# Attention: where the probabilities are divided by their sum

## The chip, the cores and the metric

The kernel runs on one core of one Trainium2 chip. Its time is the device time of one execution in microseconds (us). Beside the times stands one profiled execution, taken by the hardware profiler; its rows are used below. The engines are named as the profile names them: PE (TensorE matmul; PEld is its weight load), DVE (VectorE), ACT (ScalarE), POOL (GpSimd) and SP, which issues the weight transfers. Each engine works through its own instructions in the order in which the program holds them, and an instruction that waits holds back everything behind it on that engine.

## What is computed

Two blocks are chained over one sequence of 256 tokens with 1024 features. The first has convolutions and a mixture of experts; the change doesn't touch it. The second has two layers, each a feed-forward part, a mixer with three attentions of eight heads ("a" dilated, "b" banded with a sink, "c" over selected keys), and another feed-forward part. The step that the change touches is the same in all three attentions:

```python
p = jnp.exp(s - m[..., None])
den = p.sum(-1)
if sink is not None:
    den = den + jnp.exp(sk - m)
o = jnp.einsum('nbgrqk,nbkgd->nbqgrd', p.astype(v.dtype), vb, ...)
o = o / den.transpose(0, 1, 4, 2, 3)[..., None]
```

## The kernel before

The weights come from memory in 1 MB units through a helper that splits each into a high and a low half of 16 bits: ACT writes the high half (L120, 128x2048), DVE the low half (L107). The large projections run on PE with those halves (L1592, three terms).

In a mixer the projections of one layer come one after the other in a fixed list, and after the matmuls of each projection one **turn** of attention work is issued. The order in a turn is written out by hand: the projection's matmuls (L1592), the ACT half of the next weight unit (L120), work left over from an earlier turn (`flush`, L1768 and L1770), what the projection's result needs (`take`: the rotation on DVE, L1740 to L1743, and a copy to 16 bits on ACT, L1751), then `tick`, then the DVE half of the weight unit (L107), then `settle`. For the narrow projections `kc` and `kb` the ACT half comes after `take` and not before it.

An **item** is one attention, one block of 128 queries (c = 0 or 1) and four heads. There are 12 items in a layer, 24 in all; an item of the second query block (c = 1) has 256 keys in place of 128, so twice the probabilities. An item goes through four steps, spread over three turns:

- `soft`: scores on PE (L1840), addition of the mask on DVE into `pq` (L1893), row maximum (L1895), its negative `nm` (L1900), the exponentials on ACT in place, with their sums into `den` (L1902). `pq` lies with the queries on the partitions.
- `settle`, at the end of the same turn: the reciprocal of `den` on DVE (L1919).
- `flip`, in the next turn: transposes of `pq` on PE (L1930), their copy to `pT` on ACT (L1931), and four matmuls that spread the reciprocals over the rows of the values (L1937), copied to `div` on ACT (L1940).
- `values`, in the turn after: the matmuls with the values (L1954), the product with `div` on DVE into `o` (L1960), its high half `oh` on ACT (L1962), its low half `ol` on POOL (L1963).

`tick` issues `values` of the oldest item, `flip` of the middle one and `soft` of a new one, in this order. So on PE a flip's transposes stand after the values' matmuls and before the scores of the next item.

Of the kernel before, what the change touches and what calls it, by code (L numbers as in the profile page):

```python
# [10 lines left out]
F32 = mybir.dt.float32  # L11
# [3 lines left out]
AF = mybir.ActivationFunctionType  # L15
OP = mybir.AluOpType
# [3 lines left out]
P = 128  # L20
# [5 lines left out]
XS = 4.0  # L26
# [141 lines left out]
class Kernel:  # L168
# [958 lines left out]
    def experts(self, l, rank, w2, lp, later):  # L1127
# [111 lines left out]
        for j in range(17):  # L1239
            if j < 16:  # L1240
                pg = first("g", j)
                if j > 1:
                    scatter(j - 2)
                if j:
                    flip(j - 1)
                else:
                    back(0)
                pu = first("u", j)
                s = mp.tile([P, 512], F32, name="sil")
                nc.scalar.activation(s, pg, AF.Silu)  # L1250
                hid[j] = mp.tile([P, 512], F32, name="hid")
                nc.vector.scalar_tensor_tensor(hid[j], pu, WS[j // 2][:, j % 2 : j % 2 + 1], s, op0=OP.mult, op1=OP.mult)  # L1252
            else:
                scatter(j - 2)
                flip(j - 1)
# [448 lines left out]
class Attention:  # L1704
# [179 lines left out]
    def soft(self, x, c, hs):  # L1884
        nc, pool, kn = self.nc, self.pool, self.kn
        den = pool.tile([P, 4], F32, name="den", bufs=4)
        nm = pool.tile([P, 4], F32, name="nm", bufs=4)
        bias = self.sel[c] if x == "c" else kn.bias[x, c]
        kof = {"a": lambda h: h, "b": lambda h: h // 4, "c": lambda h: 0}[x]
        banks, nk, per = self.scores("q" + x, "k" + x, c, hs, kof)  # L1890
        pq = pool.tile([P, 4, S], F32, name="pq", bufs=3)[:, :, :nk]
        for n, bank in enumerate(banks):
            nc.vector.tensor_tensor(pq[:, n * per : n * per + per], bank.rearrange("p (j s) -> p j s", j=per),  # L1893
                                    bias[:, None].to_broadcast([P, per, nk]), op=OP.add)
        nc.vector.tensor_reduce(nm, pq, axis=AX.X, op=OP.max)  # L1895
        if x == "b":
            nc.vector.scalar_tensor_tensor(nm, nm, SOFT, self.sink[:, hs : hs + 4], op0=OP.mult, op1=OP.max)
            nc.vector.tensor_scalar(nm, nm, -1.0, None, op0=OP.mult)
        else:
            nc.vector.tensor_scalar(nm, nm, -SOFT, None, op0=OP.mult)  # L1900
        for j in range(4):
            nc.scalar.activation(pq[:, j], pq[:, j], AF.Exp, scale=SOFT, bias=nm[:, j : j + 1],  # L1902
                                 accum_out=den[:, j : j + 1])
        sk = None
        if x == "b":
            sk = pool.tile([P, 4], F32, name="sk", bufs=4)
            nc.vector.tensor_add(sk, self.sink[:, hs : hs + 4], nm)
            nc.scalar.activation(sk, sk, AF.Exp)
        self.state[x, c, hs] = (pq, den, sk)
        self.open = (den, sk)  # L1910

    def settle(self):

        if self.open:
            den, sk = self.open
            self.open = None
            if sk is not None:
                self.nc.vector.tensor_add(den, den, sk)
            self.nc.vector.reciprocal(den, den)  # L1919

    def flip(self, x, c, hs):

        nc, pool, kn = self.nc, self.pool, self.kn
        pq, den, sk = self.state[x, c, hs]
        out = []
        for s in range(c + 1):
            pt = kn.acc()
            pT = pool.tile([P, 512], F32, name="pT", bufs=4)
            for j in range(4):
                nc.tensor.transpose(pt[:, j * P : j * P + P], pq[:, j, s * P : s * P + P], kn.ident)  # L1930
            nc.scalar.activation(pT, pt, AF.Copy)  # L1931
            out.append(pT.rearrange("p (i e q) -> p i e q", e=2, q=P))

        pt = kn.ps()
        for j in range(4):
            i, e = divmod(j, 2)
            nc.tensor.matmul(pt[64 * e : 64 * e + 64, i * P : i * P + P], den[:, j : j + 1].to_broadcast([P, 64]), kn.ident,  # L1937
                             start=True, stop=True)
        div = pool.tile([P, 2 * P], F32, name="div", bufs=2)
        nc.scalar.activation(div, pt[:, : 2 * P], AF.Copy, scale=XS)  # L1940
        self.state[x, c, hs] = (out, div)

    def values(self, x, c, hs):

        nc, pool, kn = self.nc, self.pool, self.kn
        pT, div = self.state.pop((x, c, hs))
        v = self.v[x]
        pt = kn.ps()
        n = 1 if x == "a" else 2
        for i in range(0, 2, n):  # L1950
            for s in range(c + 1):
                for e in range(2):
                    v0 = {"a": (hs + 2 * i + e) * 64, "b": hs // 4 * 64, "c": 0}[x]
                    nc.tensor.matmul(pt[64 * e : 64 * e + 64, i * P : (i + n) * P].rearrange("p (i q) -> p i q", i=n),  # L1954
                                     v[:, s, v0 : v0 + 64], pT[s][:, i : i + n, e], start=(s == 0), stop=(s == c))
        if (c, hs) == (0, 0):
            self.oT[x] = tuple(pool.tile([P, 4, S], F16, name=n, bufs=2) for n in ("oh", "ol"))
        h, lo = (t[:, hs // 2 : hs // 2 + 2, c * P : c * P + P] for t in self.oT[x])
        o = pool.tile([P, 2 * P], F32, name="o", bufs=2)
        nc.vector.tensor_tensor(o, pt[:, : 2 * P], div, op=OP.mult)  # L1960
        o = o.rearrange("p (i q) -> p i q", i=2)
        nc.scalar.activation(h, o, AF.Copy)  # L1962
        nc.gpsimd.tensor_tensor(lo, o, h, op=OP.subtract)  # L1963


@with_exitstack
# [48 lines left out]
```

## Time and profile before

| | us |
|---|---|
| median of 3 runs | 2457.27 (2452.61 to 2458.95) |
| the profiled execution, its own time | 2455.99 |
| span of its trace, first to last instruction | 2454.3 |
| PE busy, of the span | 2345.2 (96%) |
| DVE busy | 1227.5 (50%) |
| ACT busy | 897.1 (37%) |
| POOL busy | 107.4 (4%) |

The two mixers lie at about 1440 to 1680 us and 2030 to 2270 us of the span. The busy shares are means over stages with different limits: what a change in the mixers is worth is read from the mixers alone, and there from which wait ends last. All times in rows are from the start of the span. A timeline row gives the start, the length, the engine, the line, the operation with what it writes and reads, and, where the engine sat idle before it, for how long and what ended that.

### The profile page before, as it was taken

What the parts mean: (1) busy time and instruction counts of PE and PEld (TensorE: products, weight loads), DVE (VectorE), ACT (ScalarE), POOL (GpSimd) and SP (SyncE); (2) the same over time, 40 slices, a digit from 0 to 9 for tenths busy, and PEclk for the clock granted to TensorE, in tenths of its full rate; (3) what the DMA queues carried; (4) which work ended last, traced back from release to release, by engine and by line L of the source; (5) the groups of instructions that cost most, each with busy time, mean ns of one, the idle gap of its engine ahead of it and who ended that gap; (6) DMA issues with size and microseconds to landing.
All of it is one profiled execution on the core that took longest, in us unless ns stands there. A gap on an engine that the chain in (4) does not pass through costs nothing.

```text
span 2454.3 us, 38061 instructions
## 1 busy us (share of the span) xinstructions
PE 2345.2 (96%) x16219; PEld 1383.2 (56%) x16219; DVE 1227.5 (50%) x1910; ACT 897.1 (37%) x1222; POOL 107.4 (4%) x169
## 2 busy tenths in 40 slices
PE   7989999999999999999979999999999999999998
PEld 5534343443386443334448855547888875554985
DVE  2775122111277222111157486968557567877654
ACT  2342111111143211111134447675444445676442
POOL 0100000000000000000020011110000002110000
PEclk8999999999999999999999999999999999999999
DMA  8977999999998999999976544536656555445651
GB/s 273 405 317 318 421 421 421 421 421 421 414 362 322 377 420 421 421 421 421 420 296 228 173 168 172 189 138 231 216 172 241 197 173 176 139 160 183 246 167 67
DMA packets 191033, 709.91 MB, mean 289 GB/s; under 512 B 15054, under 2 KB 50382, under 8 KB 134026
## 3 DMA queue, kind: packets, MB, share of 16 engines
q1 hardware_dynamic: 187850, 698.50, 73.7%
q10 hardware_dynamic: 3008, 8.92, 1.1%
q8 instruction: 129, 2.11, 0.3%
q14 instruction: 46, 0.38, 0.0%
HBM read 706.33 MB, written 1.05 MB: 288 GB/s over the span
## 4 chain that ended last, share of the span: by engine, by line
PE 50%; DMA 8%; issue 4%; DVE 4%; ACT 1%; POOL 0%; ACTq 0%; DVEq 0%; SPq 0%; POOLq 0%
PE ps L1470 18%; PE ps L1592 9%; PE ps L1198 6%; PE acc L1450 5%; DMA w<-in_e_w_up 3%; DMA w<-in_e_w_gate 3%; PE acc L1431 3%; PE ps L1220 2%; DVE w L107 1%; DMA w<-in_e_w_down 1%; PE acc L1692 1%; PE ps L1152 1%; PE ps L1954 1%; PE acc L1840 1%; PE acc L1236 1%
## 5 line engine op out<-in xcount | busy, mean ns | idle before, releaser
L107 DVE SCALAR_TENSOR_TENSOR w<-w,w 128x2048 f16<-128x2048 f32 (+3 forms) x239 | 525.6, 2213 | 234.8 <-ACT w L120 234.4
L120 ACT ACTIVATE w<-w 128x2048 f16<-128x2048 f32 (+3 forms) x239 | 434.6, 1832 | 251.5 <-PE ps L1470 140.0
L1470 PEld LDWEIGHTS <-w 128*128 128x128 f16 x4992 | 461.2, 112 | 11.4 <-issue 2.0
L1470 PE MATMUL ps<-xh,w 128*128 128x256 f16 (+1 forms) x3328 | 378.5, 257 | 1.1 <-DVE w L107 1.0
L1252 DVE SCALAR_TENSOR_TENSOR hid<-ps,ws,sil 128x512 f32<-128x512 f32 x32 | 24.0, 751 | 476.1 <-PE ps L1198 476.1
L1198 PE MATMUL ps<-w,xl 128*64 128x512 f32 x1024 | 240.4, 599 | 15.7 <-DMA w<-in_e_w_gate 15.6
L1198 PE MATMUL ps<-w,xh 128*64 128x512 f32 x1024 | 238.9, 595 | 14.8 <-DMA w<-in_e_w_gate 12.1
L1220 PE MATMUL ps<-w,hT 128*64 128x512 f32 x1024 | 237.0, 596 | 7.1 <-DMA w<-in_e_w_down 4.0
L1470 PE MATMUL ps<-xl,w 128*128 128x256 f16 (+1 forms) x1664 | 222.9, 257 | 1.9 <-DVE xl L333 1.9
L1592 PE MATMUL ps<-w,xh 128*128 128x512 f16 (+2 forms) x896 | 195.3, 362 | 0.5 <-ACT xh L332 0.5
L1198 PEld LDWEIGHTS ps<-w,xh 128*64 128x64 f32 x1024 | 80.0, 137 | 156.8 <-issue 121.2
L1198 PEld LDWEIGHTS ps<-w,xl 128*64 128x64 f32 x1024 | 78.4, 137 | 158.8 <-issue 120.1
L1220 PEld LDWEIGHTS ps<-w,hT 128*64 128x64 f32 x1024 | 80.3, 137 | 139.1 <-issue 111.0
L1227 ACT ACTIVATE yh<-y 128x512 f16<-128x512 f32 x64 | 40.3, 630 | 259.7 <-DVE y L1226 259.7
L1592 PEld LDWEIGHTS <-xh 128*128 128x128 f16 x896 | 85.4, 98 | 85.6 <-issue 2.4
L1226 DVE TENSOR_TENSOR y<-ps,g 128x512 f32<-128x512 f32 x64 | 44.0, 688 | 169.7 <-PE ps L1220 169.7
L1208 ACT ACTIVATE hT<-ps 128x512 f32<-128x512 f32 x32 | 19.1, 597 | 272.2 <-PE ps L1206 272.2
L1450 PE MATMUL acc<-w,hh 128*128 128x512 f16 x384 | 114.2, 379 | 0.0
L1592 PE MATMUL ps<-w,xl 128*128 128x512 f16 (+2 forms) x448 | 106.1, 362 | 0.0
L1431 PE MATMUL acc<-w,hh 128*128 128x512 f16 x320 | 95.2, 379 | 0.0
L1450 PE MATMUL acc<-w,hl 128*128 128x512 f16 x192 | 72.8, 379 | 0.0
L1592 PEld LDWEIGHTS <-xl 128*128 128x128 f16 x448 | 43.5, 98 | 45.7
(392 smaller groups left out, 2853.5 us busy)
## 6 DMA issues: line engine op xcount, KB each, us to landing
w<-in_e_w_gate SPq DMA_DIRECT2D x128, 1024.0 KB
w<-in_e_w_up SPq DMA_DIRECT2D x128, 1024.0 KB
w<-in_e_w_down SPq DMA_DIRECT2D x128, 1024.0 KB
w<-in_ffn_in SPq DMA_DIRECT2D x80, 1024.0 KB
w<-in_w_in SPq DMA_DIRECT2D x50, 1024.0 KB
w<-in_ffn_out SPq DMA_DIRECT2D x44, 1024.0 KB
w<-in_ada_w SPq DMA_DIRECT2D x40, 1024.0 KB
w<-in_b_w_in SPq DMA_DIRECT2D x12, 1024.0 KB
```

Of the source, the lines that this page charges most:

```text
L107: self.nc.vector.scalar_tensor_tensor(h[:, 1, :n], t[:, :n], WS, h[:, 0, :n], op0=OP.mult, op1=OP.subtract)
L120: self.nc.scalar.activation(h[:, 0, :n], t[:, :n], AF.Copy, scale=WS)
L1152: nc.tensor.matmul(pt[:, e * P : e * P + P], t[:, c, k + e :: 8], o[:, c], start=(i == c == 0), stop=(i == c == 1))
L1198: nc.tensor.matmul(pt[64 * e : 64 * e + 64], XT[j][:, 4 * h + k, 64 * e : 64 * e + 64], W[e][:, k * 512 : k * 512 + 512], start=(h == 0 an ...
L1220: nc.tensor.matmul(banks[n][64 * e : 64 * e + 64], hT[j][:, 2 * h + i, 64 * e : 64 * e + 64], W[e][:, i * D + n * 512 : i * D + n * 512 + ...
L1226: nc.vector.tensor_mul(y[:, sl], banks[n], G[:, sl])
L1227: nc.scalar.activation(yh[:, sl], y[:, sl], AF.Copy, scale=XS)
L1236: nc.tensor.matmul(accs[c][n], t, y[:, n * 512 : n * 512 + 512], start=False, stop=(j == 15 and i == 1), skip_group_check=True)
L1431: nc.tensor.matmul(accs[c][n], H[tx][:, 2 * h + f, c * P : c * P + P], ho[:, tw, f * D + n * 512 : f * D + n * 512 + 512], start=(j == 0 a ...
L1450: nc.tensor.matmul(accs[c][n], H[tx][:, 2 * h + f, c * P : c * P + P], ho[:, tw, f * D + n * 512 : f * D + n * 512 + 512], start=(j == 0 a ...
L1470: nc.tensor.matmul(pt[:, f % 2 * S + t0 : f % 2 * S + t1], h[:, tw, k * n + f : (k + 1) * n : nf], X[tx][:, 4 * (q % 2) + k, t0:t1], start ...
L1592: nc.tensor.matmul(pt[:, :n], X[tx][:, nk * q + k, c * P : c * P + P], h[:, tw, k * n : k * n + n], start=(q == 0 and k == 0 and tx == tw ...
```

## The change

The probabilities are multiplied by the reciprocals of their sums on DVE while they still lie by query, in `settle`. The four matmuls that spread the reciprocals and the copy `div` go. `oh` is then made by ACT straight from the matmuls' result, and `ol` by DVE from the same result and `oh`; the product with `div` and the subtraction on POOL go.

```diff
@@ soft
-        self.state[x, c, hs] = (pq, den, sk)
-        self.open = (den, sk)
+        self.state[x, c, hs] = pq
+        self.open = (pq, den, sk)
@@ settle
             self.nc.vector.reciprocal(den, den)
+            self.nc.vector.tensor_tensor(pq, pq, den[:, :, None].to_broadcast([P, 4, pq.shape[2]]), op=OP.mult)
@@ flip
-        pt = kn.ps()
-        for j in range(4):
-            i, e = divmod(j, 2)
-            nc.tensor.matmul(pt[64 * e : 64 * e + 64, i * P : i * P + P], den[:, j : j + 1].to_broadcast([P, 64]), kn.ident,
-                             start=True, stop=True)
-        div = pool.tile([P, 2 * P], F32, name="div", bufs=2)
-        nc.scalar.activation(div, pt[:, : 2 * P], AF.Copy, scale=XS)
-        self.state[x, c, hs] = (out, div)
+        self.state[x, c, hs] = out
@@ values
-        o = pool.tile([P, 2 * P], F32, name="o", bufs=2)
-        nc.vector.tensor_tensor(o, pt[:, : 2 * P], div, op=OP.mult)
-        o = o.rearrange("p (i q) -> p i q", i=2)
-        nc.scalar.activation(h, o, AF.Copy)
-        nc.gpsimd.tensor_tensor(lo, o, h, op=OP.subtract)
+        o = pt[:, : 2 * P].rearrange("p (i q) -> p i q", i=2)
+        nc.scalar.activation(h, o, AF.Copy, scale=XS)
+        nc.vector.scalar_tensor_tensor(lo, o, XS, h, op0=OP.mult, op1=OP.subtract)
```

On DVE, from the end of the turn that makes the second item to the mask of the third, these rows stood before (`rr`, `rq`: the rotation of the next projection; `acc`: the scores' result):

```order
L1919 RECIPROCAL den<-den 128x4
L1740 TENSOR_TENSOR rr<-ps,sind 128x8x32 x2
L1742 TENSOR_TENSOR rq<-ps,cosd 128x512
L1743 TENSOR_TENSOR rq<-rq,rr 128x512
L1960 TENSOR_TENSOR o<-ps,div 128x256
L1893 TENSOR_TENSOR pq<-acc,bias_a_9758 128x512 x2
```

The same place on DVE now:

```order
L1919 RECIPROCAL den<-den 128x4
L1920 TENSOR_TENSOR pq<-pq,den 128x4x128
L1740 TENSOR_TENSOR rr<-ps,sind 128x8x32 x2
L1742 TENSOR_TENSOR rq<-ps,cosd 128x512
L1743 TENSOR_TENSOR rq<-rq,rr 128x512
L1954 SCALAR_TENSOR_TENSOR ol<-ps,oh 128x2x128
L1893 TENSOR_TENSOR pq<-acc,bias_a_9758 128x512 x2
```

The multiplication L1920 has come in ahead of the rotation, and in the place of L1960, which read results of PE and `div`, stands L1954, which reads `oh` of ACT, ahead of the mask L1893.

On ACT, in the turn of the projection `kc` (the fourth item is made), before:

```order
L1782 ACTIVATE vc<-ps 128x64
L1783 ACTIVATE wi<-ps 128x8
L120 ACTIVATE w_11615<-w_11237 128x2048
L1962 ACTIVATE oh<-o 128x2x128
L1931 ACTIVATE pT<-acc 128x512 x2
L1940 ACTIVATE div<-ps 128x256
L1902 ACTIVATE pq,den<-pq,nm 128x256 x4
```

The same place on ACT now (L1953 is the former L1962, L1932 the former L1931):

```order
L1782 ACTIVATE vc<-ps 128x64
L1783 ACTIVATE wi<-ps 128x8
L120 ACTIVATE w_11602<-w_11237 128x2048
L1953 ACTIVATE oh<-ps 128x2x128
L1932 ACTIVATE pT<-acc 128x512 x2
L1902 ACTIVATE pq,den<-pq,nm 128x256 x4
```

`oh` stands where it stood, behind the weight's half L120, and the copy `div` is gone from between `pT` and the exponentials.

## Rows read from the trace of the kernel before

**Rows 1.** Windows of the first mixer: busy us (instructions) by engine, PEclk, DMA share, GB/s.

```profile
1440.00:1680.00 240.00, 236.57 (x1457) 126.61 (x1456) 188.42 (x307) 155.47 (x257) 37.38 (x36) 1.00 0.48 165
```

**Rows 2.** Line L1919: count, ns min/median/max, first and last start.

```profile
L1919 DVE RECIPROCAL den<-den x24: 164/178/179, 1486.1 to 2221.8; 128x4 f32<-128x4 f32 x24
```

**Rows 3.** Timeline, second and third flip of the first mixer, all engines.

```profile
1492.95 0.16 DVE L1919 RECIPROCAL den<-den 128x4 f32<-128x4 f32 x1
1493.53 0.76 DVE L1740 TENSOR_TENSOR rr<-ps,sind 128x256 f32<-128x256 f32 x2 [0.41 <-PE ps L1592]
...
1494.59 0.66 PE L1937 MATMUL ps<-ident,den 128*64 128x128 f32 x8
...
1494.92 0.69 DVE L1743 TENSOR_TENSOR rq<-rq,rr 128x512 f32<-128x512 f32 x1
...
1495.18 1.05 PE L1840 MATMUL acc<-m,T 128*128 128x256 f16 x8
...
1495.52 0.42 DVE L1960 TENSOR_TENSOR o<-ps,div 128x256 f32<-128x256 f32 x1
...
1495.72 0.63 ACT L1751 ACTIVATE h<-rq 128x512 f16<-128x512 f32 x1 [1.40 <-DVE rq L1743]
1495.86 1.28 DVE L1893 TENSOR_TENSOR pq<-acc,bias_a 128x512 f32<-128x512 f32 x2
...
1497.17 1.22 DVE L1895 TENSOR_REDUCE nm<-pq 128x4 f32<-128x1024 f32 x1
...
1498.43 0.17 DVE L1900 TENSOR_SCALAR nm<-nm 128x4 f32<-128x4 f32 x1
...
1500.74 0.18 DVE L1919 RECIPROCAL den<-den 128x4 f32<-128x4 f32 x1
...
1501.32 1.09 PE L1930 MATMUL acc<-ident,pq 128*128 128x128 f32 x8
```

**Rows 4.** Timeline, from the third to the fourth flip.

```profile
1503.99 1.27 DVE L1893 TENSOR_TENSOR pq<-acc,bias_a 128x512 f32<-128x512 f32 x2
...
1504.09 1.91 ACT L120 ACTIVATE w<-w 128x2048 f16<-128x2048 f32 x1
...
1505.89 0.41 ACT L1962 ACTIVATE oh<-o 128x256 f16<-128x256 f32 x1
...
1506.39 0.67 POOL L1963 TENSOR_TENSOR ol<-o,oh 128x256 f16<-128x256 f32 x1 [1.80 <-ACT oh L1962]
...
1506.55 0.53 DVE L1900 TENSOR_SCALAR nm<-nm 128x4 f32<-128x4 f32 x1
...
1507.42 0.53 ACT L1902 ACTIVATE pq<-pq,nm 128x256 f32<-128x256 f32 x1
...
1509.53 0.18 DVE L1919 RECIPROCAL den<-den 128x4 f32<-128x4 f32 x1 [0.26 <-ACT pq L1902]
...
1510.56 1.09 PE L1930 MATMUL acc<-ident,pq 128*128 128x128 f32 x8
```

**Rows 5.** Timeline, reciprocal and transposes of the seventh and eighth flip.

```profile
1585.51 0.18 DVE L1919 RECIPROCAL den<-den 128x4 f32<-128x4 f32 x1
...
1587.19 1.09 PE L1930 MATMUL acc<-ident,pq 128*128 128x128 f32 x8
...
1594.35 0.18 DVE L1919 RECIPROCAL den<-den 128x4 f32<-128x4 f32 x1
...
1596.43 1.09 PE L1930 MATMUL acc<-ident,pq 128*128 128x128 f32 x8
```

**Rows 6.** Timeline, reciprocal and spreading matmuls of the tenth flip.

```profile
1619.28 0.18 DVE L1919 RECIPROCAL den<-den 128x4 f32<-128x4 f32 x1
...
1619.60 0.66 PE L1937 MATMUL ps<-ident,den 128*64 128x128 f32 x8 [0.77 <-DVE den L1919]
```

**Rows 7.** Timeline of PE, a wait outside the mixers.

```profile
792.27 1.06 PE L988 MATMUL ps<-r,ones 128*128 128x32 f32 x4 [2.06 <-DVE r L984]
```

**Rows 8.** Windows, right behind that wait; columns as Rows 1.

```profile
792.00:798.50 6.50, 6.23 (x38) 4.50 (x39) 3.81 (x24) 1.80 (x5) 0.00 (x0) 0.50 0.68 245
```

More of the change, by code (lines that the diff above doesn't have):

```diff
@@ L1908, in soft @@
             nc.scalar.activation(sk, sk, AF.Exp)
-        self.state[x, c, hs] = (pq, den, sk)
-        self.open = (den, sk)
+        self.state[x, c, hs] = pq
+        self.open = (pq, den, sk)
     def settle(self):
         if self.open:
-            den, sk = self.open
+            pq, den, sk = self.open
             self.open = None
@@ L1919, in settle @@
             self.nc.vector.reciprocal(den, den)
+            self.nc.vector.tensor_tensor(pq, pq, den[:, :, None].to_broadcast([P, 4, pq.shape[2]]), op=OP.mult)
     def flip(self, x, c, hs):
         nc, pool, kn = self.nc, self.pool, self.kn
-        pq, den, sk = self.state[x, c, hs]
+        pq = self.state[x, c, hs]
         out = []
@@ L1932, in flip @@
             out.append(pT.rearrange("p (i e q) -> p i e q", e=2, q=P))
-        pt = kn.ps()
-        for j in range(4):
-            i, e = divmod(j, 2)
-            nc.tensor.matmul(pt[64 * e : 64 * e + 64, i * P : i * P + P], den[:, j : j + 1].to_broadcast([P, 64]), kn.ident,
-                             start=True, stop=True)
-        div = pool.tile([P, 2 * P], F32, name="div", bufs=2)
-        nc.scalar.activation(div, pt[:, : 2 * P], AF.Copy, scale=XS)
-        self.state[x, c, hs] = (out, div)
+        self.state[x, c, hs] = out
     def values(self, x, c, hs):
         nc, pool, kn = self.nc, self.pool, self.kn
-        pT, div = self.state.pop((x, c, hs))
+        pT = self.state.pop((x, c, hs))
         v = self.v[x]
```

## The prediction

> **What bounds the kernel now.** I read the windows of the mixers first, since the change touches nothing else. There PE is busy 236.57 of 240 us, DVE 188.42 and ACT 155.47 [rows 1]: PE sets the pace, and what is taken from PE could move the end one for one. Then I read the timeline around the flips, for the question is how much room lies between the last work on `pq` and the transposes that read it. The reader should see there that the room is small: at the third flip the reciprocal starts at 1500.74, and the transposes at 1501.32 [rows 3]; at the fourth it is 1509.53 and 1510.56 [rows 4]. The work that is put in between takes longer than that.
>
> **What goes.** From the first spreading matmul at 1494.59 to the next scores at 1495.18, a flip gives PE 0.59 us back [rows 3]. There are 24 flips [rows 2], so 24 x 0.59 = 14.2 us is the most that the change can gain. The copy `div` on ACT and the subtraction on POOL cost nothing now (nothing on PE waits for them), so dropping them gives nothing by itself.
>
> **What comes: the multiplication.** The trace has no such instruction. For 512 elements the nearest row is L1743, two inputs of the same kind, 0.69 us; for 1024 (c = 1) it is the maximum over 1024, 1.22 us [rows 3], and I take these. It can't be nothing, since every element passes through DVE; the dear bound is two L1740 pairs of 512, 2 x 0.76 = 1.52. It lies on the path twice: the transposes wait for it, and so does the rotation behind it on DVE.
>
> **What comes: `ol` on DVE.** It takes the place of L1960 at about the same price, 0.42 [rows 3]. But L1960 waited for PE alone; `ol` waits for `oh`, which stands on ACT behind L1751 or behind a weight's half of 1.91 us [rows 3, 4]. Behind `ol` on DVE stands the mask, and from there row maximum, `nm`, exponentials, reciprocal and multiplication follow one another up to the next flip. POOL had paid for that wait (1.80 us [rows 4]) without holding anybody.
>
> **The walk.** Let D be how much later than before PE stands. At each flip D grows by the wait of the transposes and falls by 0.59. An instruction starts 0.03 after the one that it waits for; without a wait, the next starts some 0.09 (DVE) or 0.11 (ACT) before the end of the one ahead, as L1743 and L1960, or L120 and `oh`, show [rows 3, 4].
>
> *First and second flip*, worked like the next: waits of 0.48 and 0.13, D = 0.61 - 1.18 = -0.57. DVE is 0.17 late.
>
> *Third.* The second item's reciprocal ends at 1493.11 + 0.17 = 1493.28, its multiplication at 1494.00, so the rotation starts at 1493.91 instead of 1493.53: +0.38. L1751 then runs 1496.10 to 1496.73, `oh` 1496.62 to 1497.03, `ol` 1497.06 to 1497.48, and the mask starts at 1497.39 instead of 1495.86: +1.53 [rows 3]. The chain carries this on: reciprocal 1500.74 + 1.53 = 1502.27 to 1502.45, multiplication to 1503.70, transposes at 1503.73. PE is there at 1501.32 - 0.57 = 1500.75 and waits 2.98. D = +1.82.
>
> *Fourth.* The narrow rotations stood right behind the reciprocal (from 1500.83) and now stand behind the multiplication (from 1503.61): +2.78. ACT's L120 moves with them to 1506.87, `oh` runs 1508.67 to 1509.08, `ol` to 1509.53, and the mask starts at 1509.44: +5.45. L1900 moves to 1512.00; it took 0.53 here beside POOL's subtraction and 0.17 without [rows 3, 4], so 0.17. Exponentials from 1512.20, reciprocal 2.11 behind them (1507.42 to 1509.53 before) at 1514.31, multiplication to 1515.74, transposes at 1515.77. PE is there at 1512.38: wait 3.39, D = +4.62. Until the items of "c" no flip follows, and D is only carried.
>
> *Fifth and sixth*: 0.25 and 0.20, D = +3.89. *Seventh*: the mask is 1.38 late beyond the carried 4.62, for the same two causes; reciprocal 1585.51 + 6.00 = 1591.51, multiplication to 1592.94, PE there at 1587.19 + 3.89 = 1591.08 [rows 5]: wait 1.89, D = +5.19. *Eighth*: with rotations and L120 in between as at the fourth, the reciprocal is 8.24 late, the multiplication ends at 1604.02, PE is there at 1601.62 [rows 5]: wait 2.43, D = +7.03. *Ninth*: 0.75, D = +7.19.
>
> *Tenth.* PE waited 0.77 for the reciprocal already [rows 6]. Now the mask of this item is 0.47 late through `oh` and `ol`, the reciprocal ends at 1619.93, the multiplication at 1620.65, and the transposes (0.58) come behind it and no longer ahead: next scores at 1621.26 instead of 1620.19 (1619.60 + 0.59), over the 7.03 carried: D = +8.10, a wait of 1.50. *Eleventh*, the same with 1024 elements: 2.26. *Twelfth*: 0.40. The rows of the six small waits and of the eleventh are like those shown.
>
> The waits add up to 16.66, the matmuls give back 12 x 0.59 = 7.08: +9.58 for a mixer, +19.2 for both (the last reciprocal of the second, at 2221.8 [rows 2], stands behind the same pattern).
>
> **The clock.** After one wait of 2.06 us PE was granted 0.50 for the 6.5 us from 792.00 to 798.50 [rows 7, 8], 1.2 GHz in place of 2.4, which can cost half of that, 3.25 us, if nothing else makes PE wait meanwhile. In both mixers it stands at 1.00 now [rows 1]. Four of the new waits of a mixer are longer than that one (2.98, 3.39, 2.43, 2.26). What is lost behind the first of them falls into the second, and part of what is lost behind the third into the waits after it. I take one full fall in the two mixers together, 3.25, or a half in each; the bounds are 0 and 4 x 3.25 = 13.0. The Trainium skill's page "TensorE: Matmul & The Clock Gate", section "Why this matters for your kernels", speaks against this change: it wants no idle gaps of PE between bursts of matmuls, for the clock drops to half. The trace agrees by that one wait; by the rule taken strictly every long wait costs, which is the rival on the clock below.
>
> **The port.** L1900 grew from 0.17 to 0.53 beside POOL's subtraction, 0.36 us; with POOL's part gone I count it back once in a mixer. The Trainium skill's page "SBUF — State Buffer", section "SBUF: two separate sides", has DVE and GpSimd exclude each other on a shared pair of ports, which this row fits; it also says that a DVE instruction with two SBUF inputs, as the multiplication, takes part in that. If that mattered, L1743 would show it at 0.69 already.
>
> **Sum.** The profiled execution's own time is 2455.99, 1.28 below the median of 2457.27. 2455.99 + 19.2 + 3.25 = 2478.4, on the median's scale 2479.7. I say 2479.
>
> **Rivals.** *Faster*: DVE is idle a fifth of the mixers, so both new pieces might fit into gaps, and the 14.2 us be won: 2441.8. It would need the multiplication to end before PE comes, which at the third flip leaves 0.40 us behind the reciprocal's end, for 1.22; it decides below about 0.4 us. Chance 0.04.
>
> *Only the multiplication counts*: `oh` is made early enough everywhere, the mask starts where it did save for the rotation's shift. The same walk then gives waits of 1.84, 1.32, 0.74, 0.42 and 0.28 for the third, fourth, seventh, eighth and ninth flip, 9.8 in a mixer in place of 16.7, +2.7 net, 2461.4 in all. For it: ACT has 85 us free in the mixer [rows 1]. Against it: the order on ACT puts 1.91 us of L120 straight ahead of `oh`. Chance 0.12.
>
> *The clock falls at all four long waits that count*: 2455.99 + 19.2 + 13.0 = 2488.2. For it the one row, against it that a late PE meets the next wait later and shortens it. Chance 0.14.
>
> **Numbers.** The forecast has 0.66, and 0.04 is left for a mixture. What can be told from no change is about 0.3%, 7.4 us, so slower begins at 2464.6. Faster 0.04; same 0.10, most of the second rival; slower 0.86. The range runs from 2465, above the second rival, to 2489, which holds the clock's rival, and the dear multiplication (0.30 more at six flips in each mixer, 3.6) on top of the forecast.
>
> **What would show it.** In the profile of the changed kernel: PE idle ahead of the flips' transposes, ended by DVE, 10 to 17 us in a mixer, the longest at the third and fourth flip; L1920 at 0.69 and 1.22; DVE idle ahead of L1954, ended by ACT; the granted clock under 1.00 in the mixers' windows. I am wrong if the transposes find `pq` ready, if `ol` doesn't wait, or if the multiplication runs at a fraction of L1743's price.

## The result, and the profile after

| | before | changed |
|---|---|---|
| median, us | 2455.36 (2452.61 to 2458.95, 4 runs) | 2477.64 (2476.02 to 2479.11, 4 runs) |
| profiled execution, own time | 2455.99 | 2476.02 |
| span of its trace | 2454.3 | 2474.3 |

The changed kernel takes 1.009 times as long, with a 95% interval of 1.0072 to 1.0107: slower by some 22 us. The forecast was 2479, with a range of 2465 to 2489.

The page of the changed kernel, part 1, busy time by engine:

```profile
PE 2338.5 (95%) x16027; PEld 1380.6 (56%) x16027; DVE 1249.2 (50%) x1934; ACT 890.2 (36%) x1198; POOL 82.7 (3%) x145
```

PE, ACT and POOL have less to do than before and DVE has 22 us more; DVE is busy half of the span as before. Nothing in these totals says that the kernel got slower. The window of the first mixer does (columns as Rows 1):

```profile
1440.00:1680.00 240.00, 224.66 (x1323) 121.02 (x1322) 189.77 (x301) 149.11 (x241) 25.19 (x24) 0.98 0.47 157
```

PE is busy 224.66 of 240 us where it had been 236.57 [rows 1], and the granted clock is under 1.00. What PE waits for is read from its lines: first the multiplication, then `ol`, then the transposes (PE's matmuls alone), each with the idle time of its engine ahead of it (us, times) and who waited for it.

```profile
L1920 DVE TENSOR_TENSOR pq<-pq,den x24: 691/958/1226, 1487.0 to 2242.3; 128x512 f32<-128x512 f32 x12, 128x1024 f32<-128x1024 f32 x12
...
  PE acc L1931: 23.8, 18
```

```profile
L1954 DVE SCALAR_TENSOR_TENSOR ol<-ps,oh x24: 417/425/426, 1497.7 to 2251.3; 128x256 f16<-128x256 f32 x24
...
  ACT oh L1953: 50.4, 22
```

```profile
L1931 PE MATMUL acc<-ident,pq x144: 272/273/448, 1487.8 to 2244.4; 128*128 128x128 f32 x144
...
  DVE pq L1920: 23.8, 18
  ACT w L120: 2.8, 4
```

In 18 of 24 flips PE waits for the multiplication, 23.8 us in all; at the eleventh and twelfth flips the profile puts another 2.8 us down to L120. It is the same wait: L120 ends there 0.06 us behind the multiplication, and in all 24 flips the transposes start 0.15 us behind the multiplication's end. In 22 of 24 turns DVE sits idle ahead of `ol` until ACT has made `oh`, 50.4 us in all. (POOL waited for `oh` before.) Idle time of DVE at this place is not new in itself: ahead of L1960 it came to 41.6 us in 12 turns of the kernel before, ended by PE's values. And no instruction is seen to wait for `ol`. So what counts is not the 50.4 us but how late the mask behind `ol` starts.

The timeline of the changed kernel from the second to the fourth flip, which answers to [rows 3, 4]:

```profile
1493.96 0.69 DVE L1920 TENSOR_TENSOR pq<-pq,den 128x512 f32<-128x512 f32 x1
...
1494.57 0.75 DVE L1740 TENSOR_TENSOR rr<-ps,sind 128x256 f32<-128x256 f32 x2
...
1497.30 0.36 ACT L1953 ACTIVATE oh<-ps 128x256 f16<-128x256 f32 x1
...
1497.69 0.42 DVE L1954 SCALAR_TENSOR_TENSOR ol<-ps,oh 128x256 f16<-128x256 f32 x1 [1.05 <-ACT oh L1953]
1498.03 1.28 DVE L1893 TENSOR_TENSOR pq<-acc,bias_a 128x512 f32<-128x512 f32 x2
...
1502.92 0.18 DVE L1919 RECIPROCAL den<-den 128x4 f32<-128x4 f32 x1
1503.13 1.22 DVE L1920 TENSOR_TENSOR pq<-pq,den 128x1024 f32<-128x1024 f32 x1
...
1504.50 1.38 PE L1931 MATMUL acc<-ident,pq 128*128 128x128 f32 x8 [3.04 <-DVE pq L1920]
...
1507.59 1.91 ACT L120 ACTIVATE w<-w 128x2048 f16<-128x2048 f32 x1
1509.39 0.38 ACT L1953 ACTIVATE oh<-ps 128x256 f16<-128x256 f32 x1
...
1509.81 0.42 DVE L1954 SCALAR_TENSOR_TENSOR ol<-ps,oh 128x256 f16<-128x256 f32 x1 [2.57 <-ACT oh L1953]
1510.15 1.28 DVE L1893 TENSOR_TENSOR pq<-acc,bias_a 128x512 f32<-128x512 f32 x2
...
1516.68 1.06 PE L1931 MATMUL acc<-ident,pq 128*128 128x128 f32 x8 [1.92 <-DVE pq L1920]
```

Both causes stand here one after the other: the mask L1893 right behind an `ol` that waited (1.05 and 2.57 us), and the transposes right behind the multiplication.

For the whole effect I measure a mixer from the start of its first projection (L1592) to the start of the next stage (L1470). The first mixer of the kernel before, two rows of the timeline of PE:

```profile
1445.88 0.59 PE L1592 MATMUL ps<-w,xh 128*128 128x512 f16 x2
...
1683.77 0.61 PE L1470 MATMUL ps<-xh,w 128*128 128x128 f16 x8
```

The same two rows of the changed kernel:

```profile
1446.53 0.59 PE L1592 MATMUL ps<-w,xh 128*128 128x512 f16 x2
...
1693.97 0.61 PE L1470 MATMUL ps<-xh,w 128*128 128x128 f16 x8
```

That is 237.89 us before and 247.44 now. The second mixer is 237.89 and 247.71. Both together went from 475.78 to 495.15, **+19.37 us**. What of the own times lies outside the mixers is 1980.21 before and 1980.87 now; over the ten traces of the experiments it lies between 1975.7 and 1979.9 with no relation to the edit that I can see, so the lengths of the mixers tell more than single times do.

The granted clock in the changed kernel's first mixer (windows, PEclk is the third number from the end):

```profile
1506.00:1508.00 2.00, 2.00 (x10) 1.21 (x9) 1.13 (x7) 1.15 (x7) 1.39 (x6) 0.50 1.05 410
1594.00:1597.00 3.00, 3.00 (x16) 2.44 (x15) 1.18 (x6) 2.09 (x5) 1.38 (x4) 0.50 1.01 387
1628.00:1631.00 3.00, 2.57 (x12) 2.06 (x13) 2.93 (x6) 1.31 (x3) 0.00 (x0) 0.50 0.88 300
```

It falls to 0.50 (1.2 GHz in place of 2.4) at the waits of the third, seventh and tenth flip, and in the second mixer at the same three places, for 3.41 us each time.

### The profile page after: what moved, and what is told of

Its sections match the earlier page's. It is cut to its first block, busy times and chain, and to the rows that moved or that the text cites. A ratio compares the mean times of both kernels' runs of the same rounds, so it can differ in the third digit from the quotient of the medians.

```text
span 2474.3 us, 37613 instructions
## 1 busy us (share of the span) xinstructions
PE 2338.5 (95%) x16027; PEld 1380.6 (56%) x16027; DVE 1249.2 (50%) x1934; ACT 890.2 (36%) x1198; POOL 82.7 (3%) x145
## 3 DMA queue, kind: packets, MB, share of 16 engines
HBM read 706.33 MB, written 1.05 MB: 286 GB/s over the span
## 4 chain that ended last, share of the span: by engine, by line
PE 43%; DVE 10%; DMA 9%; ACT 4%; issue 1%; ACTq 0%; DVEq 0%; SPq 0%
PE ps L1470 18%; PE acc L1450 5%; PE ps L1198 5%; PE ps L1592 5%; PE acc L1431 4%; DMA w<-in_e_w_up 3%; DMA w<-in_e_w_gate 3%; DVE w L107 3%; DMA w<-in_e_w_down 2%; PE ps L1220 2%; ACT w L120 1%; PE acc L1692 1%; DVE nm L1895 1%; DVE pq L1893 1%; ACT pq L1902 1%
## 5 line engine op out<-in xcount | busy, mean ns | idle before, releaser
L120 ACT ACTIVATE w<-w 128x2048 f16<-128x2048 f32 (+3 forms) x239 | 434.5, 1832 | 252.9 <-PE ps L1470 141.6
L1470 PEld LDWEIGHTS <-w 128*128 128x128 f16 x4992 | 462.8, 112 | 11.4 <-issue 2.0
L1470 PE MATMUL ps<-xh,w 128*128 128x256 f16 (+1 forms) x3328 | 379.6, 257 | 1.1 <-DVE w L107 1.0
L1470 PE MATMUL ps<-xl,w 128*128 128x256 f16 (+1 forms) x1664 | 223.8, 257 | 1.9 <-DVE xl L333 1.9
L1592 PE MATMUL ps<-w,xh 128*128 128x512 f16 (+2 forms) x896 | 198.5, 366 | 0.7 <-ACT xh L332 0.5
L1592 PEld LDWEIGHTS <-xh 128*128 128x128 f16 x896 | 87.1, 99 | 87.7 <-issue 5.6
L1592 PE MATMUL ps<-w,xl 128*128 128x512 f16 (+2 forms) x448 | 106.1, 362 | 0.0
L1152 PEld LDWEIGHTS <-zh 128*128 128x128 f16 x512 | 53.7, 148 | 27.5 <-issue 24.2
```

Of the source, the lines that this page charges most:

```text
L120: self.nc.scalar.activation(h[:, 0, :n], t[:, :n], AF.Copy, scale=WS)
L1152: nc.tensor.matmul(pt[:, e * P : e * P + P], t[:, c, k + e :: 8], o[:, c], start=(i == c == 0), stop=(i == c == 1))
L1470: nc.tensor.matmul(pt[:, f % 2 * S + t0 : f % 2 * S + t1], h[:, tw, k * n + f : (k + 1) * n : nf], X[tx][:, 4 * (q % 2) + k, t0:t1], start ...
L1592: nc.tensor.matmul(pt[:, :n], X[tx][:, nk * q + k, c * P : c * P + P], h[:, tw, k * n : k * n + n], start=(q == 0 and k == 0 and tx == tw ...
```

## The experiments

Two theories stood at the start. *Two causes*: the transposes wait for the multiplication, and `ol`'s wait for `oh` makes the next item's mask late. *Only the multiplication*: `ol`'s wait on DVE holds nobody up. On the clock there were two more: its falls cost time, or they only shorten the wait that follows. All edits are to the changed kernel unless another is named; "mixers" is the length of both as above.

| run | median us | before, beside it | ratio (95%) | mixers, against 475.78 |
|---|---|---|---|---|
| DVE makes `o` | 2459.16 | 2455.07 | 1.0019 (1.0010 to 1.0028) | +5.40 |
| no multiplication | 2454.03 | 2455.07 | 1.0000 (0.9991 to 1.0009) | -1.82 |
| neither | 2442.76 | 2455.07 | 0.9953 (0.9939 to 0.9966) | -13.87 |
| some spare transposes | 2478.72 | 2455.07 | 1.0104 (1.0088 to 1.0120) | +23.91 |
| third turn | 2461.27 | 2455.09 | 1.0025 (1.0016 to 1.0034) | +8.43 |
| third turn, POOL | 2457.14 | 2455.09 | 1.0008 (0.9999 to 1.0017) | +1.60 |
| some items only | 2452.82 | 2455.09 | 0.9989 (0.9980 to 0.9998) | -2.47 |
| scores first | 2477.12 | 2455.09 | 1.0090 (1.0076 to 1.0104) | +21.18 |
| spare transposes at all long waits | 2472.39 | 2455.28 | 1.0068 (1.0054 to 1.0082) | +19.35 |
| changed kernel again | 2477.20 | 2455.28 | 1.0087 (1.0073 to 1.0100) | +22.63 |

**DVE makes `o`.**

```diff
-        o = pt[:, : 2 * P].rearrange("p (i q) -> p i q", i=2)
-        nc.scalar.activation(h, o, AF.Copy, scale=XS)
-        nc.vector.scalar_tensor_tensor(lo, o, XS, h, op0=OP.mult, op1=OP.subtract)
+        o = pool.tile([P, 2 * P], F32, name="o", bufs=2)
+        nc.vector.tensor_scalar(o, pt[:, : 2 * P], XS, None, op0=OP.mult)
+        o = o.rearrange("p (i q) -> p i q", i=2)
+        nc.scalar.activation(h, o, AF.Copy)
+        nc.gpsimd.tensor_tensor(lo, o, h, op=OP.subtract)
```

> The changed kernel with `values` given back its old shape: DVE takes `o` out of the matmuls' result (times XS) and waits for PE alone, ACT makes `oh` from `o`, POOL makes `ol`. The multiplication of the probabilities on DVE stays. The theory of two causes (the multiplication between reciprocal and transposes, and the mask behind `ol`'s wait for `oh`): the waits of the transposes fall to what the multiplication and the rotation's shift alone make, some 10 us in a mixer in place of 16, so a time 4 to 9 us above the kernel before, about 2461, and the long DVE waits ended by ACT's `oh` (22 of them, 50 us) are gone. The rival that only the multiplication counts: `ol`'s wait held nobody up, so no change against the changed kernel, about 2477.

The time is 4.1 us above the kernel before, as two causes wanted, and DVE waits for ACT's `oh` no longer (ahead of `o` it waits for PE, 31.7 us in 8 turns). The transposes in its trace wait for the multiplication 13.4 us in place of 23.8:

```profile
L1931 PE MATMUL acc<-ident,pq x144: 272/273/436, 1485.2 to 2227.9; 128*128 128x128 f32 x144
...
  DVE pq L1920: 13.4, 16
```

So 13.97 of the 19.37 us go with `ol` on DVE. That does not make it the larger part: the next run shows that the loss goes without the multiplication too. The mixers grow by 2.70 us each, and 2.7 is what the prediction's walk gave for the rival "only the multiplication counts": that rival's sum was right for this kernel, and wrong for the change, where `oh` is not made in time.

**No multiplication.**

```diff
             self.nc.vector.reciprocal(den, den)
-            self.nc.vector.tensor_tensor(pq, pq, den[:, :, None].to_broadcast([P, 4, pq.shape[2]]), op=OP.mult)
```

> The changed kernel without the multiplication: the output is not divided by the sums. `ol` on DVE behind `oh` stays. Two causes: `ol`'s wait alone makes the third flip wait about 1.4 us and some others less, which about eats the matmuls that were dropped; a time between 2 us below and 5 us above the kernel before, about 2457. The rival that only the multiplication counts: all of the loss goes and the 14 us of the dropped matmuls appear, about 2442.

No difference from before can be measured; the rival's 2442 is out. `ol` waits as it did:

```profile
L1954 DVE SCALAR_TENSOR_TENSOR ol<-ps,oh x24: 417/425/426, 1493.1 to 2226.5; 128x256 f16<-128x256 f32 x24
...
  ACT oh L1953: 50.5, 22
```

This wait alone eats most of what the dropped matmuls give (the run after this one measures that). The first mixer is 1.77 us shorter than before, the second only 0.05, though they hold the same program. Windows of this run, the first around the third and fourth flip of the first mixer, the second behind the fourth flip of the second:

```profile
1495.00:1515.00 20.00, 17.93 (x123) 10.38 (x122) 13.49 (x29) 15.12 (x36) 1.96 (x8) 1.00 0.30 106
2095.00:2097.00 2.00, 2.00 (x8) 1.11 (x7) 0.00 (x0) 2.00 (x2) 0.00 (x0) 0.50 0.04 8
```

The clock fell in the second mixer alone. Up to the fourth flip the two mixers run alike, and from the fifth on the second is later; the 1.71 us between them are what that fall cost.

**Neither**: both edits together.

> The multiplication left out (the output is not divided by the sums) and `values` with its old shape (DVE waits for PE alone, POOL makes `ol`): what the dropped spreading matmuls are worth by themselves. Two causes: they are on the path, so the kernel is 10 to 14 us faster than before, about 2443. A rival, that the dropped matmuls only filled waits (the transposes' copies and the scores wait anyway): within 4 us of the kernel before.

The mixers get 13.87 us shorter, and the time is 12.3 us under the kernel before, as two causes wanted. That is the worth of the dropped matmuls by themselves, 24 x 0.58, where the prediction had 14.2. Set against it in lengths of the mixers, `ol` on DVE costs 12.05 (-13.87 to -1.82; 10.34 without the fall of 1.71), the multiplication 19.27 (-13.87 to +5.40), and both together 33.24. So they are two costs and not one seen twice: `ol` alone eats most of the gain, and the multiplication alone more than all of it. Together they cost 3.6 us more than 10.34 and 19.27; no run shows where this comes from.

**Some spare transposes**, before the transposes of three flips (`self.nf` counts the flips):

```diff
+            for j in range({2: 8, 6: 5, 9: 7}.get(self.nf % 12, 0) if s == 0 else 0):
+                nc.tensor.transpose(pt[:, j % 4 * P : j % 4 * P + P], kn.ident, kn.ident)
             for j in range(4):
                 nc.tensor.transpose(pt[:, j * P : j * P + P], pq[:, j, s * P : s * P + P], kn.ident)
```

> The changed kernel with 8, 5 and 7 spare transposes of the identity (0.27 us each) ahead of the transposes of the third, seventh and tenth flip of each mixer, into the bank that the transposes then write. PE works through most of the waits of 3.04, 1.91 and 2.67 us, behind which the clock was granted at 0.50 for 3.41 us each. If the clock stays up and its fall had a price of its own, up to half of 6 x 3.41 us is won: 2467 or somewhat above. If what the fall costs only shortens the next wait (the reading of the profile), no change: within 2 us of the changed kernel, and the waits of the fourth, eighth and eleventh flip grow by what the clock gave back (1.92 to about 3.4, 0.88 to about 2.4, 1.08 to about 2.3).

No gain; but the expectation had mis-sized the spares (their starts in the trace are 0.11 us apart, not 0.27, so about two thirds of each wait were left: 2.02, 1.21 and 1.76 us) and had not seen that the falls would move. (The 0.14 of a later expectation is the stretch of eight spares, 1.09 us, over eight, with the end of the last in it.) The transposes of the third, fourth, seventh and eighth flip in this run's timeline (L1933):

```profile
1500.24 1.07 PE L1933 MATMUL acc<-ident,pq 128*128 128x128 f32 x8 [2.02 <-DVE pq L1920]
...
1512.42 1.09 PE L1933 MATMUL acc<-ident,pq 128*128 128x128 f32 x8 [3.58 <-DVE pq L1920]
...
1591.14 1.06 PE L1933 MATMUL acc<-ident,pq 128*128 128x128 f32 x8 [1.21 <-DVE pq L1920]
...
1602.26 1.94 PE L1933 MATMUL acc<-ident,pq 128*128 128x128 f32 x8 [2.54 <-DVE pq L1920]
```

Windows of the same run, behind the third, the fourth and the eighth flip:

```profile
1500.00:1506.00 6.00, 5.75 (x35) 3.56 (x36) 3.12 (x19) 3.94 (x12) 1.96 (x8) 1.00 0.94 342
1514.00:1516.00 2.00, 2.00 (x6) 0.74 (x5) 1.48 (x2) 2.00 (x5) 0.00 (x0) 0.50 0.00 0
1603.00:1605.00 2.00, 2.00 (x9) 1.39 (x8) 0.63 (x2) 2.00 (x5) 0.00 (x0) 0.50 0.00 0
```

In the first mixer the clock stays up behind the third flip; the fourth then waits 3.58 in place of 1.92, and its transposes start no earlier. There the clock falls now, and again at the eighth. In the second mixer it fell behind the third flip in spite of the spares, and at the eleventh. The mixers are 3.27 and 1.28 us longer than in the first trace of the changed kernel. The table under "spare transposes at all long waits" shows what follows from that.

**Third turn**: an item's transposes come one turn later, its values one more, `pq` has four buffers, and ACT makes `o` and `oh`, POOL `ol`.

```diff
...
+        if self.pipe[2]:
+            self.values(*self.pipe[2])
         if self.pipe[1]:
-            self.values(*self.pipe[1])
-        if self.pipe[0]:
-            self.flip(*self.pipe[0])
+            self.flip(*self.pipe[1])
...
```

> The changed kernel with a third turn in the pipe (an item's transposes come one turn later, its values one more, four buffers of `pq`), and `o` and `oh` both made by ACT, `ol` by POOL, so that DVE waits for no ACT in `values`. The multiplication on DVE then has a whole turn of slack ahead of the transposes. If what costs is only that the transposes wait for the multiplication, this brings the gain of the dropped matmuls back: about 2443. If the late work is only passed on (DVE still carries the multiplication, the copies `pT` stand behind the weights' halves on ACT, and the values come straight behind), new waits ahead of the values take its place: 2457 to 2464.

The gain does not come back: the wait for the multiplication is nearly gone (1.8 us, twice), and the values wait for `pT` in its place (PE 18.1 us, ten times), as the second theory of that expectation said. Rows of its timeline, at the third item's values:

```profile
1500.94 1.91 ACT L120 ACTIVATE w<-w 128x2048 f16<-128x2048 f32 x1
...
1503.48 0.58 ACT L1932 ACTIVATE pT<-acc 128x512 f32<-128x512 f32 x1
...
1504.12 0.66 PE L1947 MATMUL ps<-pT,va 128*64 128x128 f32 x8 [2.73 <-ACT pT L1932]
```

ACT's weight half stands ahead of the copy, and between them `o` and `oh`, which this run gave to ACT. Counted from each trace's first L1592 (1441.35 here) the weight half starts 1.38 us later than before [rows 4], though PE is earlier than before at this place: the narrow rotations, which ACT's work ahead of it waits for, come behind the multiplication on DVE.

**Third turn, POOL**: the same with `nc.gpsimd.tensor_tensor` for the multiplication.

> As the kernel with the third turn, but the multiplication is made by POOL, which is idle for nearly the whole mixer, so that DVE carries none of the new work. If the rotation behind the multiplication on DVE is what costs once the transposes have slack, the gain comes back in part: 4 to 10 us below the kernel before, about 2449. If POOL is too slow for the multiplication or DVE's share was harmless: no better than the kernel with the multiplication on DVE, 2457 or more.

Neither expectation was met: better than with DVE by 4 us, but the 4 to 10 us of gain are not there. POOL took 1.04 and 1.90 us for what DVE does in 0.69 and 1.22, and the values still wait for `pT`, 12.9 us in 6 times. The first mixer is 1.00 us shorter than before, the second 2.60 longer. In the second the clock fell, in the first it didn't:

```profile
1440.00:1680.00 240.00, 229.38 (x1370) 123.05 (x1369) 188.53 (x295) 156.68 (x259) 57.31 (x48) 1.00 0.49 163
2093.00:2095.00 2.00, 2.00 (x11) 1.85 (x10) 0.66 (x2) 2.00 (x6) 1.66 (x2) 0.50 0.00 0
2219.00:2225.00 6.00, 5.41 (x21) 3.11 (x22) 4.04 (x2) 5.97 (x10) 3.73 (x2) 0.50 0.74 272
```

**Some items only**, an edit to the kernel before: items of the first query block are multiplied on DVE and lose their spreading matmuls, save the tenth.

```diff
...
+    def early(self, x, c, hs):
+        return c == 0 and (x, hs) != ("b", 4)
...
             self.nc.vector.reciprocal(den, den)
+            if pq is not None:
+                self.nc.vector.tensor_tensor(pq, pq, den[:, :, None].to_broadcast([P, 4, P]), op=OP.mult)
...
+        if self.early(x, c, hs):
+            self.state[x, c, hs] = (out, None)
+            return
...
+        if div is None:
+            nc.vector.tensor_scalar(o, pt[:, : 2 * P], XS, None, op0=OP.mult)
+        else:
+            nc.vector.tensor_tensor(o, pt[:, : 2 * P], div, op=OP.mult)
```

> The kernel before, in which only the items of the first query block (128 keys, multiplication 0.69 us) are multiplied on DVE and lose their spreading matmuls, save the tenth; all others stay as they were, `o` is made by DVE everywhere. By the waits of the run in which DVE makes `o`, the first two flips win 0.57, the fifth and sixth 0.3 to 0.4 each, the ninth 0.3: 1.6 in a mixer, 2 to 4 us below the kernel before in all. If the late rotation behind a multiplication hits the next item's flip (the third, above all) even so: no gain, 0 to 3 us above the kernel before.

Faster than both kernels, as the first theory wanted, but by little: 2.3 us under the kernel before, with an interval of 0.5 to 4.9. The mixers are 1.23 and 1.24 us shorter, where 1.6 was expected of each. Its transposes (L1935) wait for the multiplication (L1924) 2.2 us in all:

```profile
  DVE pq L1924: 2.2, 8
```

It changes the items at which the shorter multiplication of 0.69 us ends before or soon after PE comes, and leaves the others alone.

**Scores first.**

```diff
-        if self.pipe[0]:
-            self.flip(*self.pipe[0])
         if new:
...
+        if self.pipe[0]:
+            self.flip(*self.pipe[0])
         self.pipe = [new, self.pipe[0]]
```

> The changed kernel with the next item's scores issued ahead of the transposes, so that PE has 1.05 us of work while the multiplication runs. If the waits are only a matter of order on PE, up to 1 us of each long wait is filled: 2468 or below. If the chain on DVE and ACT sets the pace, a filled wait is met again, since the transposes and the copies and values behind them come later: no gain, 2475 to 2483.

No gain, as the chain wants it. PE does the scores while the multiplication runs, and then the values, which stand ahead of everything in the next turn, wait for `pT` (L1947, idle time of PE's matmuls ahead of it):

```profile
  ACT pT L1932: 31.7, 17
```

In the changed kernel PE has no such wait; there its waits for the multiplication are 26.6 us, and here 0.6.

**Spare transposes at all long waits**: as above, with `{2: 16, 3: 18, 6: 9, 7: 12, 9: 13, 10: 10}`.

> The changed kernel with spare transposes of the identity ahead of the third, fourth, seventh, eighth, tenth and eleventh flip of each mixer (16, 18, 9, 12, 13 and 10 of them, 0.14 us apart, as the run with fewer spares showed), so that PE works through most of each long wait and no fall is only moved to the next wait. If the falls of the changed kernel cost time, the mixers get shorter by up to half of six times 3.41 us, to 485 to 490 us for both in place of 495.15. If the falls behind the third, seventh and tenth flip are all paid back by a shorter next wait, the mixers stay at 495 us, within 1, with the clock at 1.00 throughout, and the time at the changed kernel's, 2477.

The granted clock in this run over the flips of the two mixers:

```profile
1480.00:1650.00 170.00, 159.62 (x1021) 91.25 (x1020) 136.13 (x239) 109.75 (x208) 12.80 (x18) 1.00 0.43 146
2070.00:2250.00 180.00, 169.43 (x1086) 96.48 (x1084) 138.68 (x242) 116.81 (x214) 12.94 (x19) 1.00 0.46 156
```

With no fall at all the mixers take 495.13 us, against 495.15 in the first trace of the changed kernel with its six falls: those six cost nothing. And yet the median is 4.8 us under that of the changed kernel on the same chip (2471.74 to 2473.12 against 2474.77 to 2478.73), where the second theory had the two alike. The mean granted clock of a whole execution is 0.987 or 0.988 in these five (0.986 to 0.988 in the kernel before) and 0.982 to 0.985 in the five of the changed kernel. The next run shows how the two go together.

**The changed kernel again.**

> The changed kernel once more, beside the same runs of the kernel before, for a narrower interval: 2475 to 2480, 0.8 to 1.0% above the kernel before. The forecast without its clock term is 19.2 us, the one with it 22.4; the mixers' own lengths in the first trace gave 19.4.

The ratio is that of the first measurement. In this trace the falls lie elsewhere, behind the third, fourth, seventh and tenth flip of the first mixer and behind the fourth of the second. Windows behind the two fourth flips:

```profile
1516.00:1518.00 2.00, 2.00 (x6) 0.73 (x5) 1.29 (x2) 2.00 (x5) 0.00 (x0) 0.50 0.00 0
...
2113.00:2116.00 3.00, 3.00 (x12) 2.11 (x12) 1.05 (x2) 3.00 (x7) 0.00 (x0) 0.50 0.02 5
```

The mixers are 249.12 and 249.29 us long, 1.68 and 1.58 more than in the first trace. How late the transposes start against [rows 3 to 5], each trace counted from its own first L1592:

| flip | predicted (D + 0.59) | changed | with spares at all waits | with some spares | changed again |
|---|---|---|---|---|---|
| third | 2.41 | 2.53 | 2.53 | 2.52 | 2.53 |
| fourth | 5.21 | 5.47 | 5.46 | 5.46 | 5.47 |
| seventh | 5.78 | 5.87 | 5.86 | 7.55 | 7.56 |
| eighth | 7.62 | 7.75 | 7.74 | 9.43 | 9.45 |

The transposes of the run with spares at all waits, and below them those of the changed kernel again, from which its columns come:

```profile
1501.43 1.07 PE L1933 MATMUL acc<-ident,pq 128*128 128x128 f32 x8 [1.15 <-DVE pq L1920]
...
1513.60 1.06 PE L1933 MATMUL acc<-ident,pq 128*128 128x128 f32 x8 [1.47 <-DVE pq L1920]
```

```profile
1514.61 1.22 PE L1931 MATMUL acc<-ident,pq 128*128 128x128 f32 x8 [2.27 <-DVE pq L1920]
...
1593.33 1.43 PE L1931 MATMUL acc<-ident,pq 128*128 128x128 f32 x8 [1.91 <-DVE pq L1920]
```

The third and fourth flip of the second mixer of the changed kernel again, where the clock did not fall behind the third:

```profile
2100.67 1.06 PE L1931 MATMUL acc<-ident,pq 128*128 128x128 f32 x8 [3.05 <-DVE pq L1920]
...
2112.84 1.94 PE L1931 MATMUL acc<-ident,pq 128*128 128x128 f32 x8 [3.59 <-DVE pq L1920]
```

A fall behind the third flip (first trace) leaves the fourth where it was: what PE lost there comes off the next wait, which the multiplication ends at the same time in any case. A fall behind the fourth (the last two columns) stands in every later row with 1.7 us; the next flip comes 60 us later, and its wait is as short as without the fall (0.21). With some spares the falls at the eighth and at the eleventh flip cost 1.6 and 1.3 more. The lost time is the same; whether it costs anything depends on what waits next. In the run in which DVE makes `o` the clock fell behind the third and tenth flip of the first mixer and behind the third of the second, and both are 240.59 us long.

## Why the prediction was right

- **What goes**: 14.2 us at most; the run without both additions measures 13.87.
- **The multiplication** was priced at 0.69 and 1.22; L1920 took 0.691 and 1.226. The dear bound of 1.52 is out.
- **`ol`** took 0.42 as priced, and waited for `oh` in 22 turns.
- **The walk**: with the 0.65 that the changed trace starts later taken off, the third item's rotation starts at 1493.92 (predicted 1493.91), its mask at 1497.38 (1497.39), its reciprocal at 1502.27 (1502.27); the fourth item's mask at 1509.50 (1509.44). The transposes are 0.1 to 0.3 later than predicted at the four flips of the table; 0.12 of it is that they start 0.15 behind the multiplication and not 0.03. Both mixers together: +19.37, predicted 19.2.
- **The waits one by one** were right where PE comes at full clock (3.04 for 2.98 at the third flip, 1.91 for 1.89 at the seventh), and too long behind a fall (1.92 for 3.39 at the fourth). The tenth waits 2.67, not 1.50: the 1.50 was PE's added lateness. From the old transposes (1617.86) to the spreading matmuls (1619.60 [rows 6]) PE had 1.74 us and needed 0.58; the other 1.16 stands ahead of the transposes now. All of PE's waits are 26.6 us (23.8 + 2.8) in place of 33.3, since PE at half clock is itself longer at work. None of this moves the sum. The second mixer of the changed kernel again, at full clock up to the fourth flip and again behind that fall, has the waits of the walk: 3.05, 3.59, 1.91, 2.54 and 2.52 at the third, fourth, seventh, eighth and eleventh flip, for 2.98, 3.39, 1.89, 2.43 and 2.26.
- **The clock** is the one term that was right by luck. The reason given for less than every fall, that what is lost behind one wait falls into the next, holds. But the price of a fall was twice too high: the row that it was taken from had the clock at 0.50 for 6.5 us, in the mixers it stood there for 3.41 us at a time, and where this cost anything it cost 1.6 to 1.7. One fall at 3.25 was counted for both mixers; the first trace had six that cost nothing, the second five, of which two cost 3.26 together (1.68 and 1.58). So the second trace's mixers are 22.63 longer than before, for the 22.4 of the sum with this term, and the first trace's 19.37, for the 19.2 without it. Two traces don't give a mean. The bound of 13.0 took four falls that count, though a mixer has four long waits and the two have eight; it did not say why half of them. The rival on the clock (13.0) is out all the same. Nor does the length of a wait tell where the clock falls, as the choice of waits longer than 2.06 us took it: it fell at waits of 1.91 us (the seventh flip), and in the second mixer of the changed kernel again not at 3.05 and 2.67. The Trainium skill's page "TensorE: Matmul & The Clock Gate", section "Why this matters for your kernels", wants no idle gaps between bursts of matmuls. The traces agree so far that each of the eleven falls in the mixers of the changed kernel's two traces comes at or behind a flip's wait; they show besides that not every such wait brings a fall, and that a fall ahead of another wait is free.
- **The port**: L1900 in the fourth turn took 0.17 at 1512.72, without POOL's subtraction beside it, as counted. The prediction had one row for this; the traces bear it out throughout (see the last section). L1743's row could not tell whether it bears on the multiplication, for POOL stood still beside it; L1920 itself took 0.69 or 1.22 to 1.23 in all 24 turns.
- **The medians**: 22.3 us lie between them; the forecast lay 21.7 above the median of three runs that it started from, 2457.27, which a fourth run brought down to 2455.36.
- **The rival "only the multiplication counts"** failed on its condition: `oh` is not made early. Its time was right for the kernel in which DVE makes `o`.

Left open is how the 4.8 us between the last two medians split over falls in the mixers and the scatter of the stages outside, which no edit here touches; in the two traces 3.28 of 4.21 us lie in the mixers.

## What to carry to other kernels

Work that is moved off the busiest engine onto a half idle one costs nothing only if it lands where nobody is waiting: read the slack between the last writer and the first reader at each place, and price the new instruction against that and not against the engine's busy share. An instruction that takes an operand from another engine's queue (`ol` behind `oh`) brings that queue's lateness to everything behind it: 24 instructions of 0.42 us cost some 10 us here, in the place of others as long, so ask first what stands ahead of its operand. Where the slack differs from item to item, make the change for the items that have it: of the kernels here that compute the whole result, that one alone beat both, if only by 2.3 us.

## What the runs showed of the hardware

- Two executions of the same program had the clock at 0.50 at different places (at the third, seventh and tenth flip of both mixers in one; at these and the fourth of the first mixer and at the fourth alone of the second in the other), and differed in the mixers by 3.26 us.
- A fall behind the fourth flip cost 1.58 to 1.71 us in four mixers of three kernels; behind the third, seventh and tenth of the changed kernel, with another wait to come, nothing.
- Transposes of a constant kept the granted clock at 1.00 in both mixers, at waits that are up to 3.59 us long without them, and the kernel with this useless work was 4.8 us faster than without. About half as many, at three of the six waits, did not keep it there.
- L1900, an instruction of DVE on 128x4 elements, took 0.17 us wherever POOL stood still, and 0.47 to 0.64 wherever POOL was at work as it started; it then ended some 0.02 us behind POOL's instruction. This is so in all 64 of its executions in the traces of the kernel before, the changed kernel, the one in which DVE makes `o` and the third turn with POOL.
